# Up projections of block 1's gated FFNs with seven block products for eight, in a three-block decoder on one core

## The chip, the cores and the metric

One NeuronCore of a Trainium2 chip runs the whole program once. The metric is the device time of one execution in microseconds (us). The engines have their own queues: TensorE (PE, with its weight loads PEld), VectorE (DVE), ScalarE (ACT), GpSimd (POOL) and SyncE (SP), which here issues the loads of the weights. Each queue is worked off in its order. Results of TensorE land in banks of 128 partitions x 2 KB (PSUM); everything else works on SBUF.

## The reference, cut to what matters

Three blocks follow each other on 512 tokens of 1024 features, in the first block with 16 memory tokens ahead of them (528). Block 1 has two gated FFNs, one on 528 tokens and one on 512:

```
def swiglu(x, w_in, w_out):
    a, b = jnp.split(x @ w_in, 2, axis=-1)
    return (jax.nn.silu(a) * b) @ w_out

h = h + 0.5 * swiglu(rmsnorm(h, norm_ffn1), w_ffn1_in, w_ffn1_out)
...
h = h + 0.5 * swiglu(rmsnorm(h, norm_ffn2), w_ffn2_in, w_ffn2_out)
```

`w_in` is 1024 x 5632 and `w_out` 2816 x 1024: 22 pairs of gate and value blocks of 128 features each.

## The kernel before, in words

Features lie on partitions, tokens along the free axis. A residual stream of 8 tiles `h` [128, T] stays in SBUF. Each fp32 operand of a large product is split into a hi part in float32r (ScalarE, `activation Copy`) and a lo part, the rest (VectorE, `tensor_sub`), and a product is three matmuls: hi x hi, hi x lo, lo x hi (`mm3`, L248 to L252).

`wunit` (L232) loads a weight block of 128 output features, [128, 8 chunks, 128], on SP's queue (L239), and splits it: ScalarE L240, VectorE L244. Its three tiles have two buffers each. `block` (L258) runs one such unit over all chunks and, for 528 tokens, over two halves of 264 columns into two banks; for 512 tokens into one. There are eight banks.

`make_z` (L891) makes `zh`, `zl`, the split of `h` times the norm's gain. The norm's factor per token, `rs`, is made by `rstd` (L336) from sums of squares and is applied to the result of a projection, so the matmuls needn't wait for it.

`swiglu` (L369) goes over 22 pairs. For each, two blocks a (gate) and b (value); then for each half: VectorE multiplies a by `rs` (L380), ScalarE takes Silu (L381), GpSimd multiplies by `rs` (L382), VectorE multiplies by b (L384), and the result is split into `hh`, `hl` of that pair (L282, L287). After the loop, the down projection takes 8 output blocks over 22 chunks of `hh`, `hl`, and `done` (L928) adds half of it to `h`. The two blocks of pair 0 are issued ahead of `rs` (`ahead`, L254).

No order is written out by hand. The framework's scheduler takes the instructions in program order with their dependencies, and gives each engine a fixed order, in which one that is ready may go ahead of an earlier one that isn't; each engine then keeps that order on the chip. Buffers are handed on tile by tile.

Of the kernel before, what the change touches and what calls it, by code (L numbers as in the profile page):

```python
# [102 lines left out]
def arrays1(I, vec):  # L103
    """layouts for the first block"""
# [92 lines left out]
class Ctx:  # L197
# [13 lines left out]
    def psum(self, mm, s=0, t=0, o=0):  # L211
        """the banks: for projections, scores, transposes, and sums over several steps"""
# [19 lines left out]
    def wunit(self, src, kc, m=P):  # L232
        """src: DRAM AP [128, kc*m]; gives hi, lo tiles [128, kc, m]."""
# [60 lines left out]
    def stacked(self, out, x, s):  # L294
        """rows 64 s .. of x: hi parts in the same rows of out, lo parts in the other half"""
# [5 lines left out]
    def twice(self, hi, lo, x, s):  # L301
        """hi and lo parts of rows 64 s .. of x, each on both halves"""
# [7 lines left out]
    def unstack(self, out, ps):  # L310
        """the two halves of a bank added"""
# [13 lines left out]
    def sq_acc(self, acc, h, first, scale=1.0):  # L325
        """acc += (h * scale)^2"""
# [9 lines left out]
    def rstd(self, acc, halves, eps, name, pool=None, factor=None):  # L336
        """rstd of the columns, times factor if there is one, on all partitions: exp(-ln(mean + eps) / 2)"""
# [31 lines left out]
    def swiglu(self, w_up, w_dn, zs, rs, halves, hid, done):  # L369
        """w_up: DRAM [44, 128, 1024] with blocks a0 b0 a1 b1 ..; w_dn: [8, 128, 22*128]."""  # L370
        nc = self.nc
        T = rs.shape[1]
        for f in range(DFF):
            pa = self.block([(w_up[2 * f], KC)], zs, halves, key=2 * f)
            pb = self.block([(w_up[2 * f + 1], KC)], zs, halves, key=2 * f + 1)
            hh, hl = hid[f]
            for (s, z), a, b in zip(halves, pa, pb):
# [5 lines left out]
                tb = self.tp.tile([P, 512], F32, name="tb")[:, :z]  # L383
                nc.vector.tensor_mul(tb, b, ta)  # L384
                self.split(hh[:, c], hl[:, c], tb)
# [49 lines left out]
    def rstd_mm(self, sq, ones, eps, pool, name, psum=None):  # L435
        """exp(-ln(ones^T sq + eps) / 2), sq [128, <=512] fp32 (overwritten)"""
# [14 lines left out]
    def newton(self, r, ms, eps, u, spread=True):  # L451
        """one step for r ~ 1 / sqrt(ms + eps); u is scratch; spread: on three engines"""
# [11 lines left out]
    def head_sq(self, t, pool, bufs=2):  # L464
        """squares, and their hi and lo parts"""
# [8 lines left out]
    def head_fin(self, sq, halves, eps, pool, bufs=2, spread=False):  # L474
        """1 / sqrt of each head's mean"""
# [23 lines left out]
def act_tables(nc):  # L499
    """loads ScalarE's table sets where a function needs another one: the set that serves the most functions ahead"""  # L500
# [29 lines left out]
def mixer1(K, D, hs, zs, rs, work):  # L530
    """D: dict of DRAM APs and constant tiles. Gives mixed hi/lo (8 tiles, 512 tokens)."""
# [18 lines left out]
    def gate(n):  # L550
        """the projection of an output gate (0 .. of the attention, 8 .. of the retention, 16 .. of its output), kept in DRAM"""
# [17 lines left out]
    fst = ExitStack()  # L569
    ya = mb  # L570
    with tc.tile_pool(name="fox", bufs=1, reuse_waits="tile") as fp:
# [24 lines left out]
        def prep(j, res):  # L596
            """the operands of pair j, in stages"""
# [34 lines left out]
        def scores(j, s, ops):  # L632
            """softmax over each query tile's keys"""
# [49 lines left out]
        def forget(pf):  # L683
            """minus the cumulative sum of log_sigmoid, per head: the logarithms token-major, the memory last"""
# [206 lines left out]
def make_z(K, hs, gain, acc, T0=0, more=None, sq=True):  # L891
    """z = h * gain as hi/lo, and acc = sum of squares over the row blocks"""
# [19 lines left out]
def block1(K, D, tables):  # L912
# [9 lines left out]
    def ffn(zs, rs, halves, up, dn, T0):  # L922
        T = rs.shape[1]
        with tc.tile_pool(name="hid", bufs=1, reuse_waits="tile") as pool:
            hid = [(pool.tile([P, T], F32R, name=f"hh{f}"), pool.tile([P, T], F32R, name=f"hl{f}"))
                   for f in range(DFF)]

            def done(n, pl):  # L928
                for (s, z), p in zip(halves, pl):
# [1070 lines left out]
```

## Time and profile before

| what | value |
|---|---|
| median of 3 runs | 3465.2 us (3464.43 to 3467.01) |
| span of the profiled execution | 3469.6 us |
| the profiled execution's own time | the page gives the span alone |
| instructions | 45531 |
| matmuls | 17777 |
| HBM read | 288.22 MB |

The profile is of one execution. Its span runs from the first to the last instruction and stands 4.4 us above the median of the runs. Instructions are counted with their line in the kernel; a helper's line gathers many callers. "Idle before" names what ended the wait of an engine.

### The profile page before, as it was taken

What the parts mean: (1) busy time and instruction counts of PE and PEld (TensorE: products, weight loads), DVE (VectorE), ACT (ScalarE), POOL (GpSimd) and SP (SyncE); (2) the same over time, 40 slices, a digit from 0 to 9 for tenths busy, and PEclk for the clock granted to TensorE, in tenths of its full rate; (3) what the DMA queues carried; (4) which work ended last, traced back from release to release, by engine and by line L of the source; (5) the groups of instructions that cost most, each with busy time, mean ns of one, the idle gap of its engine ahead of it and who ended that gap; (6) DMA issues with size and microseconds to landing.
All of it is one profiled execution on the core that took longest, in us unless ns stands there. A gap on an engine that the chain in (4) does not pass through costs nothing. (4 is left out here: it accounts for less than half of the span.)

```text
span 3469.6 us, 45531 instructions
## 1 busy us (share of the span) xinstructions
PE 3344.1 (96%) x17777; PEld 2764.7 (80%) x17777; DVE 1955.4 (56%) x3248; ACT 1416.7 (41%) x2474; POOL 755.8 (22%) x786
## 2 busy tenths in 40 slices
PE   8999999999999999999999999999989998999999
PEld 7999977878777888867777778888878776768887
DVE  4443366656654443278776664666366656766642
ACT  3222366643333222245554333444334434654431
POOL 2211133321112111112211321111234432421100
PEclk9999999999999999999999999999999988999999
DMA  3323222232133333333332323333330012123233
GB/s 121 89 91 90 87 81 74 74 104 92 59 95 97 95 94 93 96 92 94 92 100 85 114 89 92 94 95 96 113 95 26 23 47 80 41 60 97 94 101 94
DMA packets 89590, 298.63 MB, mean 86 GB/s; under 512 B 10711, under 2 KB 11351, under 8 KB 89120
## 3 DMA queue, kind: packets, MB, share of 16 engines
q1 hardware_dynamic: 76896, 260.70, 24.5%
q0 software_dynamic: 6416, 23.80, 2.4%
q10 hardware_dynamic: 6064, 11.23, 1.0%
q8 instruction: 139, 2.28, 0.3%
q14 instruction: 75, 0.61, 0.1%
HBM read 288.22 MB, written 7.47 MB: 85 GB/s over the span
## 5 line engine op out<-in xcount | busy, mean ns | idle before, releaser
L250 PE MATMUL mm<-zh,wh 128*128 128x512 f32 (+1 forms) x3296 | 1187.4, 360 | 20.1 <-ACT zh L291 8.7
L252 PE MATMUL mm<-zh,wl 128*128 128x512 f32 (+1 forms) x3296 | 1190.1, 361 | 3.3 <-DVE wl L244 3.2
L251 PE MATMUL mm<-zl,wh 128*128 128x512 f32 (+1 forms) x3296 | 1182.7, 359 | 4.2 <-DVE zl L292 4.2
L240 ACT ACTIVATE wh<-w 128x1024 fp32r<-128x1024 f32 (+2 forms) x523 | 523.7, 1001 | 1088.7 <-PE mm L251 771.1
L244 DVE TENSOR_TENSOR wl<-w,wh 128x1024 fp32r<-128x1024 f32 (+2 forms) x523 | 626.1, 1198 | 400.0 <-ACT wh L240 391.1
L250 PEld LDWEIGHTS mm<-zh,wh 128*128 128x128 f32 x3296 | 621.8, 189 | 117.3 <-issue 9.1
L251 PEld LDWEIGHTS mm<-zl,wh 128*128 128x128 f32 x3296 | 623.1, 189 | 103.6 <-DVE zl L292 5.1
L252 PEld LDWEIGHTS mm<-zh,wl 128*128 128x128 f32 x3296 | 622.8, 189 | 95.8 <-DVE wl L244 6.4
L250 PE MATMUL mm<-hh,wh 128*128 128x512 f32 (+1 forms) x880 | 308.7, 351 | 0.0
L251 PE MATMUL mm<-hl,wh 128*128 128x512 f32 (+1 forms) x880 | 308.5, 351 | 0.0
L252 PE MATMUL mm<-hh,wl 128*128 128x512 f32 (+1 forms) x880 | 307.9, 350 | 0.0
L252 PEld LDWEIGHTS mm<-hh,wl 128*128 128x128 f32 x880 | 165.7, 188 | 23.3
L251 PEld LDWEIGHTS mm<-hl,wh 128*128 128x128 f32 x880 | 165.7, 188 | 23.1
L250 PEld LDWEIGHTS mm<-hh,wh 128*128 128x128 f32 x880 | 165.7, 188 | 23.1
L382 POOL TENSOR_TENSOR ta<-ta,rs 128x264 f32<-128x264 f32 (+1 forms) x66 | 85.9, 1314 | 395.7 <-ACT ta L381 395.7
L334 POOL TENSOR_TENSOR acc<-acc,ta 128x512 f32<-128x512 f32 (+1 forms) x49 | 83.4, 1703 | 350.3 <-ACT ta L333 349.9
L1000 POOL TENSOR_TENSOR cv<-cv 128x512 f32<-128x512 f32 x44 | 57.5, 1306 | 436.3 <-DVE cv L981 398.8
L981 DVE SCALAR_TENSOR_TENSOR cv<-ta,vec,cv 128x510 f32<-128x510 f32 (+1 forms) x176 | 132.0, 753 | 3.1 <-ACT cv L978 0.3
L384 DVE TENSOR_TENSOR tb<-mm,ta 128x264 f32<-128x264 f32 (+1 forms) x66 | 32.8, 519 | 142.1 <-PE mm L252 138.3
L995 DVE TENSOR_TENSOR ta<-mm,rs 128x512 f32<-128x512 f32 x88 | 60.3, 687 | 59.6 <-PE mm L252 59.5
L380 DVE TENSOR_TENSOR ta<-mm,rs 128x264 f32<-128x264 f32 (+1 forms) x66 | 32.5, 518 | 107.8 <-PE mm L252 107.8
L282 ACT ACTIVATE hh<-cv 128x512 fp32r<-128x512 f32 x44 | 27.8, 633 | 144.1 <-POOL cv L1000 144.1
(596 smaller groups left out, 4829.1 us busy)
## 6 DMA issues: line engine op xcount, KB each, us to landing
w<-in_w_up_dram SPq DMA_DIRECT2D x176, 512.0 KB, 3.5
w<-in_w_in_dram SPq DMA_DIRECT2D x160, 512.0 KB, 3.5
w<-in_w_dn_dram SPq DMA_DIRECT2D x64, 512.0 KB, 3.5
w<-in_w_dn_dram SPq DMA_DIRECT2D x32, 384.0 KB, 3.1
w<-in_w_out_dram SPq DMA_DIRECT2D x16, 512.0 KB, 3.6
aB<-acum_d POOLq DMA_DIRECT2D x16, 512.0 KB, 6.0
w<-in_w_pb_dram SPq DMA_DIRECT2D x32, 256.0 KB, 3.0
negc<-negc_d POOLq DMA_DIRECT2D x8, 528.0 KB, 4.1
```

What stands on the lines that cost most here:

```text
L240: nc.scalar.activation(h_, w_, AF.Copy)
L244: nc.vector.tensor_sub(l_, w_, h_.bitcast(F32))
L250: nc.tensor.matmul(ps, wh, xh, start=start, stop=False)
L251: nc.tensor.matmul(ps, wh, xl, start=False, stop=False)
L252: nc.tensor.matmul(ps, wl, xh, start=False, stop=stop)
L334: nc.gpsimd.tensor_tensor(acc, acc, q, op=ALU.add)
L380: nc.vector.tensor_mul(ta, a, rs[:, c])
L382: nc.gpsimd.tensor_tensor(ta, ta, rs[:, c], op=ALU.mult)
L384: nc.vector.tensor_mul(tb, b, ta)
L981: nc.vector.scalar_tensor_tensor(y[:, d:], x[:, :T - d], w(i), y[:, d:], op0=ALU.mult, op1=ALU.add)
L995: nc.vector.tensor_mul(x, p, rs)
L1000: nc.gpsimd.tensor_tensor(y[1], y[1], y[0], op=ALU.mult)
```

## The change

The value of 19 of the 22 pairs is computed as a 2x2 block product in seven products (Winograd's form of Strassen's method). The 2x2 blocks: rows are the gate block a and the value block b, the inner dimension is cut in chunks 0 to 3 and 4 to 7, columns are the left and the right half of the tokens (264 or 256 columns). Each product is 4 chunks x 3 matmuls.

- The first three pairs (`ords=3`) stay as they are, except that the result is stored as fp32 and not split.
- `combos(k)`: for chunk k and k + 4, `h` times gain times `rs` (so the norm's factor is now inside), as four quarters in `F`, then four subtractions on GpSimd, then the split of seven pieces. It is called for k = 0 to 3 in the course of the first two ordinary pairs.
- `weights(f)`: loads a and b of the pair (two DMAs, a tile `b32` more with two buffers), makes their combinations `s12` (GpSimd) and `s34` (half VectorE, half GpSimd), and splits a whole unit of a, `s12`, `s34` and half a unit of b.
- `fast(f)`: seven products P1 to P7 into three banks a, b, c, with partial results added in between by VectorE (`w`, `y`, the right value `x_R`, the right gate, the left value) and ScalarE (a copy, two Silu), and gate times value on GpSimd at the end. In the prediction `x_R` is the addition after P5, which reads bank b before P7 adds to it; u0 to u3 are the weights of P1 and P4, P2 and P3, P5 and P6, P7.
- The results of all 22 pairs stay in fp32, in the tiles that held `zh`, `zl` and in six more. After the loop they are split, all 22, into tiles that lie where the scratch of the fast pairs was; then the down projection goes as before.
- Docstrings and comments are taken out elsewhere in the file, which shifts no instruction.

```
-    def swiglu(self, w_up, w_dn, zs, rs, halves, hid, done):
-        for f in range(DFF):
+    def swiglu(self, w_up, w_dn, zs, rs, hs, gain, done, ords=3):
+        hp = pool(left, "hx")
+        seven = ExitStack()
+        bp = pool(seven, "b32")
+        cz = pool(seven, "cz")
...
+        def ordinary(f):
             pa = self.block([(w_up[2 * f], KC)], zs, halves, key=2 * f)
             pb = self.block([(w_up[2 * f + 1], KC)], zs, halves, key=2 * f + 1)
-            hh, hl = hid[f]
+            x = tile_of(f)
             for (s, z), a, b in zip(halves, pa, pb):
                 c = slice(s, s + z)
                 ta = self.tp.tile([P, 512], F32, name="ta")[:, :z]
                 nc.vector.tensor_mul(ta, a, rs[:, c])
                 nc.scalar.activation(ta, ta, AF.Silu)
                 nc.gpsimd.tensor_tensor(ta, ta, rs[:, c], op=ALU.mult)
-                tb = self.tp.tile([P, 512], F32, name="tb")[:, :z]
-                nc.vector.tensor_mul(tb, b, ta)
-                self.split(hh[:, c], hl[:, c], tb)
+                nc.vector.tensor_mul(x[:, c], b, ta)
+            return x
+
+        def combos(k, fp):
+            F = fp.tile([P, 8, h], F32, name="F", bufs=2)
+            v = lambda x: x.rearrange("p (a b) -> p a b", a=2)
+            for n, o in ((k, F[:, 0:8:7]), (k + 4, F[:, 1:3])):
+                nc.vector.scalar_tensor_tensor(o, v(hs[n]), gain(n), v(rs), op0=ALU.mult, op1=ALU.mult)
+            for o, x, y in ((3, 7, 0), (4, 2, 3), (5, 2, 7), (6, 1, 4)):
+                nc.gpsimd.tensor_tensor(F[:, o], F[:, x], F[:, y], op=ALU.subtract)
+            zh = cz.tile([P, 7, h], F32R, name=f"ch{k}")
+            zl = cz.tile([P, 7, h], F32R, name=f"cl{k}")
+            self.split(zh, zl, F[:, :7])
+            ck.append((zh, zl))
+
+        def weights(f, sp):
+            wa = self.wp.tile([P, KC, P], F32, name="w32", bufs=2)
+            wb = bp.tile([P, KC, P], F32, name="b32", bufs=2)
+            nc.sync.dma_start(wa.rearrange("p a b -> p (a b)"), w_up[2 * f])
+            nc.sync.dma_start(wb.rearrange("p a b -> p (a b)"), w_up[2 * f + 1])
+            u0 = [self.wp.tile([P, KC, P], F32R, name=n) for n in ("wh", "wl")]
+            split_unit(u0, wa)
+            s12 = sp.tile([P, KC, P], F32, name="s12")
+            s34 = sp.tile([P, KC, P], F32, name="s34")
+            sub = lambda o, x, y, op=ALU.subtract: nc.gpsimd.tensor_tensor(o, x, y, op=op)
+            sub(s12[:, :4], wb[:, :4], wb[:, 4:], ALU.add)
+            sub(s12[:, 4:], s12[:, :4], wa[:, :4])
+            u1 = [sp.tile([P, KC, P], F32R, name=n, bufs=2) for n in ("uh", "ul")]
+            split_unit(u1, s12)
+            nc.vector.tensor_sub(s34[:, :4], wa[:, :4], wb[:, :4])
+            sub(s34[:, 4:], wa[:, 4:], s12[:, 4:])
+            u2 = [sp.tile([P, KC, P], F32R, name=n, bufs=2) for n in ("uh", "ul")]
+            split_unit(u2, s34)
+            u3 = [self.wp.tile([P, KC, P], F32R, name=n)[:, :4] for n in ("wh", "wl")]
+            split_unit(u3, wb[:, 4:])
+            return u0, u1, u2, u3
+
+        def product(ps, u, at, b, first):
+            for k in range(4):
+                wh, wl = u[0][:, at + k], u[1][:, at + k]
+                xh, xl = ck[k][0][:, b], ck[k][1][:, b]
+                kw = dict(skip_group_check=True)
+                nc.tensor.matmul(ps, wh, xh, start=first and k == 0, stop=False, **kw)
+                nc.tensor.matmul(ps, wh, xl, start=False, stop=False, **kw)
+                nc.tensor.matmul(ps, wl, xh, start=False, stop=k == 3, **kw)
+
+        def fast(f, sp):
+            u0, u1, u2, u3 = weights(f, sp)
+            a, b, c = (self.pp.tile([P, 512], F32, name="mm")[:, :h] for _ in range(3))
...
+            product(a, u0, 0, 0, True)
+            nc.scalar.activation(m, a, AF.Copy)
+            product(b, u1, 4, 4, True)
+            nc.vector.tensor_add(w, b, m)
+            product(c, u1, 0, 3, True)
+            nc.vector.tensor_add(y, c, m)
+            product(a, u0, 4, 1, False)
+            nc.scalar.activation(g[:, lr[0]], a, AF.Silu)
+            product(b, u2, 0, 5, False)
+            nc.vector.tensor_add(x[:, lr[1]], b, y)
+            product(c, u2, 4, 2, False)
+            nc.vector.tensor_add(g[:, lr[1]], c, w)
+            nc.scalar.activation(g[:, lr[1]], g[:, lr[1]], AF.Silu)
+            product(b, u3, 0, 6, False)
+            nc.vector.tensor_add(x[:, lr[0]], b, m)
+            nc.gpsimd.tensor_tensor(x, x, g, op=ALU.mult)
+            return x
+
+        with tc.tile_pool(name="F", bufs=1, reuse_waits="tile", side="right") as fp:
+            for f in range(ords):
+                xs.append(ordinary(f))
+                if f < 2:
+                    combos(2 * f, fp)
+                    combos(2 * f + 1, fp)
+        sp = pool(right, "sw", "right")
+        for f in range(ords, DFF):
+            xs.append(fast(f, sp))
+        right.close()
+        seven.close()
+        h0, h1 = pool(right, "hr", "right"), pool(left, "hl")
+        hid = []
+        for f in range(DFF):
+            hid.append([(h0 if f < 8 else h1).tile([P, T], F32R, name=f"h{e}{f}") for e in "hl"])
+            self.split(*hid[f], xs[f])
         for n in range(KC):
             d = w_dn[n]
             pn = self.block([(d[:, :1024], 8), (d[:, 1024:2048], 8), (d[:, 2048:], 6)], hid, halves)
             done(n, pn)
...
-    ffn(zs, rs, H2, D["w_up1"], D["w_dn1"], 0)
+    ffn(zs, rs, H2, D["w_up1"], D["w_dn1"], 0, lambda n: V("norm_ffn1", n))
...
-    ffn(zs, rs, [(0, 512)], D["w_up2"], D["w_dn2"], 16)
+    ffn(zs, rs, [(0, 512)], D["w_up2"], D["w_dn2"], 16, lambda n: V("norm_ffn2", n))
```

## Rows read from the trace of the kernel before

**Rows 1.** The page, busy us of each engine, share of the span and count.

```profile
PE 3344.1 (96%) x17777; PEld 2764.7 (80%) x17777; DVE 1955.4 (56%) x3248; ACT 1416.7 (41%) x2474; POOL 755.8 (22%) x786
```

**Rows 2.** Stretches of the two up phases: length, busy us of PE PEld DVE ACT POOL, clock.

```profile
58.10:279.00 220.90, 220.90 (x1826) 220.90 (x1825) 89.74 (x152) 64.11 (x114) 41.71 (x38) 1.00 0.30 91
1133.00:1344.00 211.00, 211.00 (x915) 171.44 (x914) 84.86 (x97) 61.57 (x78) 34.03 (x19) 1.00 0.31 95
```

**Rows 3.** Timeline of VectorE, L380 19 pairs apart (start us, us, engine, line).

```profile
52.29 0.79 DVE L380 TENSOR_TENSOR ta<-mm,rs 128x264 f32<-128x264 f32 x2 [2.57 <-PE mm L252]
...
273.20 0.79 DVE L380 TENSOR_TENSOR ta<-mm,rs 128x264 f32<-128x264 f32 x2 [2.52 <-PE mm L252]
...
1137.72 0.69 DVE L380 TENSOR_TENSOR ta<-mm,rs 128x512 f32<-128x512 f32 x1 [2.44 <-PE mm L252]
...
1348.49 0.69 DVE L380 TENSOR_TENSOR ta<-mm,rs 128x512 f32<-128x512 f32 x1 [2.81 <-PE mm L252]
```

**Rows 4.** Waits of PE from 1070 to 1470 us, all there are.

```profile
PE mm L250 <- DVE h L956: 0.9, 1, 0.9
```

**Rows 5.** Timeline of PE, three matmuls of 256 columns in a row.

```profile
856.60 0.37 PE L250 MATMUL s<-rqh,rkh 128*128 128x256 f32 x1
856.80 0.28 PE L251 MATMUL s<-rql,rkh 128*128 128x256 f32 x1
856.92 0.28 PE L252 MATMUL s<-rqh,rkl 128*128 128x256 f32 x1
```

**Rows 6.** Lengths: groups by form (mean ns), and by tile or line (shortest/median/longest ns).

```profile
L240 ACT ACTIVATE wh<-w 128x1024 fp32r<-128x1024 f32 x440 | 465.2, 1057 | 916.2 <-PE mm L251 667.8 <-issue 229.6 <-DMA w<-in_w_in_dram 11.3
L282 ACT ACTIVATE hh<-tb 128x512 fp32r<-128x512 f32 x22 | 13.9, 632 | 2.1 <-DVE tb L384 2.1
L287 DVE TENSOR_TENSOR hl<-tb,hh 128x512 fp32r<-128x512 f32 x22 | 15.0, 684 | 0.7 <-ACT hh L282 0.7
...
L244 DVE TENSOR_TENSOR wl<-w,wh x523: 293/1225/2370, 10.2 to 3456.6; 128x1024 fp32r<-128x1024 f32 x147, 128x512 fp32r<-128x512 f32 x19, 128x768 fp32r<-128x768 f32 x8, 128x256 fp32r<-128x256 f32 x1
L384 DVE TENSOR_TENSOR tb<-mm,ta x66: 431/433/692, 36.6 to 1354.1; 128x264 f32<-128x264 f32 x44, 128x512 f32<-128x512 f32 x22
L382 POOL TENSOR_TENSOR ta<-ta,rs x66: 741/1486/1797, 35.9 to 1350.0; 128x264 f32<-128x264 f32 x44, 128x512 f32<-128x512 f32 x22
```

**Rows 7.** Timelines of VectorE and GpSimd, operations that meet and ones that don't.

```profile
1349.39 1.23 DVE L244 TENSOR_TENSOR wl<-w,wh 128x1024 fp32r<-128x1024 f32 x1 [0.21 <-ACT wh L240]
1349.98 1.80 POOL L382 TENSOR_TENSOR ta<-ta,rs 128x512 f32<-128x512 f32 x1 [9.30 <-ACT ta L381]
...
1076.89 1.87 DVE L292 SCALAR_TENSOR_TENSOR zl<-h,vec,zh 128x512 fp32r<-128x512 f32 x1
1076.92 1.29 POOL L334 TENSOR_TENSOR acc<-acc,ta 128x512 f32<-128x512 f32 x1 [11.43 <-ACT ta L333]
...
1082.49 0.75 DVE L292 SCALAR_TENSOR_TENSOR zl<-h,vec,zh 128x512 fp32r<-128x512 f32 x1
```

**Rows 8.** Timeline of VectorE: rs finished (L462), third pair's last bank read (L384).

```profile
34.15 0.77 DVE L462 SCALAR_TENSOR_TENSOR rs<-ta,rs 128x264 f32<-128x264 f32 x2
...
58.16 0.79 DVE L384 TENSOR_TENSOR tb<-mm,ta 128x264 f32<-128x264 f32 x2 [3.26 <-PE mm L252]
...
1125.58 0.69 DVE L462 SCALAR_TENSOR_TENSOR rs<-ta,rs 128x512 f32<-128x512 f32 x1
...
1143.33 0.69 DVE L384 TENSOR_TENSOR tb<-mm,ta 128x512 f32<-128x512 f32 x1 [3.49 <-PE mm L252]
```

**Rows 9.** Timeline of PE after a wait, and that stretch's row (columns of rows 2).

```profile
33.26 0.22 PE L1349 MATMUL mm<-oh,rb 33*8 33x16 f32 x2 [1.67 <-DVE ta L460]
33.57 0.59 PE L250 MATMUL mm<-zh,wh 128*128 128x264 f32 x1
...
36.37 0.36 PE L250 MATMUL mm<-zh,wh 128*128 128x264 f32 x1
...
30.00:40.00 10.00, 8.24 (x48) 6.70 (x47) 5.69 (x13) 4.33 (x12) 1.99 (x3) 0.83 0.20 56
```

More of the change, by code (lines that the diff above doesn't have):

```diff
@@ L366, in eps, with pool, tile_of @@
         return self._eps[v]
-    def swiglu(self, w_up, w_dn, zs, rs, halves, hid, done):
-        nc = self.nc
+    def swiglu(self, w_up, w_dn, zs, rs, hs, gain, done, ords=3):
+        nc, tc = self.nc, self.tc
         T = rs.shape[1]
-        for f in range(DFF):
+        h = T // 2
+        lr = [slice(0, h), slice(h, T)]
+        left, right = ExitStack(), ExitStack()
+        def pool(st, name, side="left"):
+            return st.enter_context(tc.tile_pool(name=name, bufs=1, reuse_waits="tile", side=side))
+        hp = pool(left, "hx")
+        seven = ExitStack()
+        bp = pool(seven, "b32")
+        cz = pool(seven, "cz")
+        def tile_of(f):
+            i = f - ords
+            if 0 <= i < 16:
+                return self.zp.tile([P, 528], F32, name=f"z{'hl'[i % 2]}{i // 2}")[:, :T]
+            return hp.tile([P, T], F32, name=f"hx{f}")
+        def ordinary(f):
+            halves = [(0, h), (h, h)] if T > 512 else [(0, T)]
             pa = self.block([(w_up[2 * f], KC)], zs, halves, key=2 * f)
             pb = self.block([(w_up[2 * f + 1], KC)], zs, halves, key=2 * f + 1)
-            hh, hl = hid[f]
+            x = tile_of(f)
             for (s, z), a, b in zip(halves, pa, pb):
@@ L382, in swiglu @@
                 nc.gpsimd.tensor_tensor(ta, ta, rs[:, c], op=ALU.mult)
[L383 to L385 removed]
+                nc.vector.tensor_mul(x[:, c], b, ta)
+            return x
+        ck = []
+        def combos(k, fp):
[9 more added lines that the diff above has]
+            ck.append((zh, zl))
@@ new lines, in split_unit @@
+        def split_unit(hl, x):
+            r = "p a b -> p (a b)"
+            self.split(hl[0].rearrange(r), hl[1].rearrange(r), x.rearrange(r))
+        def weights(f, sp):
[19 more added lines that the diff above has]
+            return u0, u1, u2, u3
@@ new lines, in product @@
+        def product(ps, u, at, b, first):
[9 more added lines that the diff above has]
+            a, b, c = (self.pp.tile([P, 512], F32, name="mm")[:, :h] for _ in range(3))
+            x = tile_of(f)
+            g = self.tp.tile([P, 528], F32, name="ta")[:, :T]
+            m = sp.tile([P, 264], F32, name="m1", bufs=2)[:, :h]
+            wx = self.tp.tile([P, 528], F32, name="tb")[:, :T]
+            w, y = wx[:, :h], wx[:, h:]
+            product(a, u0, 0, 0, True)
[15 more added lines that the diff above has]
+            return x
@@ new lines, in swiglu @@
+        xs = []
+        with tc.tile_pool(name="F", bufs=1, reuse_waits="tile", side="right") as fp:
[10 more added lines that the diff above has]
+        h0, h1 = pool(right, "hr", "right"), pool(left, "hl")
@@ L386, in swiglu @@
+        hid = []
+        for f in range(DFF):
+            hid.append([(h0 if f < 8 else h1).tile([P, T], F32R, name=f"h{e}{f}") for e in "hl"])
+            self.split(*hid[f], xs[f])
+        halves = [(0, h), (h, h)] if T > 512 else [(0, T)]
         for n in range(KC):
@@ L389, in swiglu @@
             done(n, pn)
+        right.close()
+        left.close()
     def setup_consts(self, c):
@@ L920, in block1, with ffn, done @@
         nc.sync.dma_start(hs[n], D["x"][n])
-    def ffn(zs, rs, halves, up, dn, T0):
+    def ffn(zs, rs, halves, up, dn, T0, gain):
         T = rs.shape[1]
[L924 to L929, printed above, removed]
-                    c = hs[n][:, T0 + s:T0 + s + z]
-                    nc.vector.scalar_tensor_tensor(c, p, 0.5, c, op0=ALU.mult, op1=ALU.add)
-            K.swiglu(up, dn, zs, rs, halves, hid, done)
+        def done(n, pl):
+            for (s, z), p in zip(halves, pl):
+                c = hs[n][:, T0 + s:T0 + s + z]
+                nc.vector.scalar_tensor_tensor(c, p, 0.5, c, op0=ALU.mult, op1=ALU.add)
+        K.swiglu(up, dn, zs, rs, [h[:, T0:T0 + T] for h in hs], gain, done)
     acc = new_acc(K, 528)
```

## The prediction

> **What bounds the kernel now.** Read first the busy times, then the stretches of the two up phases, then their repetition, then who waits. TensorE is busy 96% of the span, VectorE 56%, GpSimd 22% [rows 1]. In both up phases TensorE is busy in the whole of its stretch at granted clock 1.00, that is at 2.4 GHz, while VectorE stands at 40% and GpSimd below 20% [rows 2]. So the time of these phases is a count of matmuls times their distance. The same step of a pair recurs 19 pairs apart at 52.29 and 273.20 us in the first FFN, at 1137.72 and 1348.49 us in the second [rows 3]: 220.91 / 19 = 11.627 us and 210.77 / 19 = 11.093 us a pair. Over 96 matmuls of 264 columns that is 0.1211 us each, over 48 of 512 columns 0.2311 us. From 1070 to 1470 us TensorE has one wait, of 0.9 us, ahead of the second up phase [rows 4]; the wait before the first ends at 33.26 us [rows 9]. No wait is there to be won; only columns are.
>
> **Columns.** A fast pair issues 7 products x 4 chunks x 3 = 84 matmuls of half the tokens; 19 of 22 pairs are fast. First FFN: 84 x 0.1211 = 10.17 us, a gain of 1.45 us a pair, 27.6 us in 19. Second FFN: 256 columns lie near 264, and the line through 0.1211 and 0.2311 us gives 0.1176 us; three such matmuls in a row started 0.12 us apart [rows 5]. At 0.119 a pair costs 10.0 us and gains 1.09, 20.7 us in all; the ends are 0.1176 (23.0 us) and 0.1211 (17.5 us). I take 20: **-47.6 us** together.
>
> **New work beside it, per fast pair.** Lengths are undisturbed ones [rows 6]. ScalarE: three hi parts at 1.06, one of half width at 0.63, a copy and two Silu of half the tokens, under 0.63 each: 5.7 us. VectorE: three lo parts at 1.225, one at 0.69, half of s34 at 0.69, five additions out of banks at 0.43: 7.2 us. GpSimd: three combinations of 512 columns and one product x*g at 1.29 [rows 7]: 5.2 us. Each alone is under 10 us. But two of them meet. A VectorE lo part from 1349.39 to 1350.62 makes a GpSimd product begun at 1349.98 last 1.80 us, where another of its size took 1.29; and a VectorE scaling begun just ahead of a GpSimd addition took 1.87 us, where the same beside none takes 0.75 [rows 7]. So the later of the two waits for the earlier when both read SBUF twice. The bank additions, with one SBUF operand, show none of this: 0.43 at the shortest and in the median. What must share is then 3 x 1.225 + 2 x 0.69 = 5.06 us of VectorE and 5.16 of GpSimd: 10.2 us of recorded length against 10.17 of TensorE. The overlap of the pair at 1349.39 (2.39 us where the lengths add to 2.52) takes 5% off: 9.7 us. It fits, narrowly. The Trainium skill's page "SBUF — State Buffer", section "Who interferes with whom", states the same as a rule: a two-SBUF-input VectorE instruction and a GpSimd one that reads SBUF exclude each other wholly. By that rule the sum would be 10.2 us and TensorE would just lose its lead; the 1.80 us agrees with it but for the 5%.
>
> Laying one pair out by these lengths (products of 1.45 us, P1 at 0, P4 ending at 5.8): u0's buffer is free at 5.8; Silu, then its hi part end at 7.5; its lo part, behind one addition and one GpSimd operation, ends near 9.0, needed at 10.15. The addition x_R follows P5 at 7.25 and frees bank b by 7.7, needed by P7 at 8.7. u1 has 4.8 us to spare, u2 likewise. So no wait when the order suits; I book 0.1 us a pair, **+4 us**. The ends are 0 and 0.75 (below, the second rival).
>
> The DMAs are the same blocks (two of 512 KB a pair) on SP's queue, now every 10.2 us for 11.6, with two buffers more; the queue gets ahead of need, at no cost. If it didn't, each pair would wait for a block.
>
> **The start of the fast pairs.** Product 1 needs all four combos and these need rs. First FFN: rs is done at 34.92 us, the third ordinary pair leaves TensorE at 58.16: a window of 23.2 us. Second: 1126.27 to 1143.33, 17.1 us [rows 8]. Work that shares the port until then: GpSimd 16 subtractions of half the tokens at 0.74 [rows 6] and three ordinary products, 15 us; VectorE eight scalings at 0.75 [rows 7], four lo parts of 1848 columns (by the line through 512 and 1024 columns 2.09 each), three weight parts at 1.225: 18 us. Undivided 33 us, with 5% off 31. The need is 1.1 us after the window. The first FFN would be late by 6.6 us, the second by 13. Lower ends by VectorE alone (18 and 5 of bank work, 23 us): 0 to 1 and 5 to 6. Part of GpSimd's 15 us falls beside the 5 us of bank work, so I take 5 and 10. After a wait of 1.67 us TensorE ran 13 matmuls 0.22 us apart in place of 0.12 (33.57 to 36.37 us, granted clock 0.83 in that stretch: 1.2 GHz for a part of it) [rows 9]; 13 x 0.1 = 1.3 us, here taken as 1.5 each. **+18 us**, ends 8 and 26.
>
> **The hand-over to the down projection.** Before, each pair's split ran inside the loop. Now 22 splits stand after it, 22 x 0.68 = 15 us of VectorE and 22 x 0.63 = 14 of ScalarE [rows 6], ahead in the code of the first down weights. Some ten can run in the last pair, as its scratch comes free; then the down phase eats a split per 0.7 us. Weights for its second unit, needed 5.8 us in, wait for u3's buffers and stand behind twelve splits (12 x 0.68 + 1.225 = 9.4 us): 3.6 us late, with the slower clock 5. Lower end 0, if those weights go first. I take 4 each, **+8 us**, ends 0 and 13. What leaves the pairs, 44 halves of splits, was hidden and gives nothing.
>
> **Sum.** -47.6 + 4 + 18 + 8 = -17.6 us on a profiled span of 3469.6, 3452.0. That span is 4.4 us above the median of the runs, 3465.2; so **3447.6 us**. Its own ends, with 512-to-256 columns, start and hand-over: about 3437 to 3458.
>
> **Rivals.** (1) *All hidden*: order and overlap cover start and hand-over to some 5 us; 3465.2 - 47.6 + 5 = 3423. For it: VectorE is at 40%. Against it: the 17.1 us window. Chance 0.17. (2) *x_R behind a lo part*: VectorE's queue keeps its order, and if u0's lo part stands before x_R, it ends at 8.95, x_R at 9.4, and P7 waits 0.7 us in each of 38 pairs; 28 for the 4 booked: 3472. Chance 0.20. (3) *Slower: the port becomes the bound.* If the bank additions (2.1 us a pair) also stand still whenever VectorE's queue waits for GpSimd, a pair takes up to 7.2 + 5.2 = 12.4 us; halfway to 10.2 it is 11.3, that is 0.3 less than before in the first FFN and 0.2 more in the second: the gain is gone, start and hand-over remain, 3465.2 + 26 - 2 = 3489, and at 12.4 some 3530. It decides from (11.36 - 26/38) = 10.7 us a pair. The rule of the skill's page pulls to this side. Chance 0.20. (4) *No fewer columns' worth of time*: 84 matmuls for 48 in the second FFN would break even at 11.093 / 84 = 0.132 us each; the 0.12 of [rows 5] speaks against it. With the first FFN alone gaining: 3465.2 - 27.6 + 30 = 3468. Chance 0.03. The forecast keeps 0.40.
>
> **Numbers.** The measurement tells about 0.2%, 7 us, from no change. Faster by more (under 3458): nearly all of the forecast, all of rival 1, a little of 2: 0.58. Same: 0.15, mostly of rival 2. Slower (over 3472): 0.27, rival 3 and half of 2. Range 3424 to 3495: it leaves out half of rival 1 and the upper half of rival 3.
>
> **What would show it.** Right: up phases busy throughout, a pair recurring every 10.2 and 10.0 us, one gap of 5 to 10 us ahead of each first fast pair ended by VectorE's lo part of the last combo, and a gap of some 4 us early in each down phase. Rival 2: a short wait in every pair for the addition x_R. Rival 3: pairs over 10.7 us, VectorE operations at twice their length beside GpSimd, TensorE waiting for lo parts. Wrong altogether if the time moves outside block 1's FFNs.

## The result, and the profile after

The median is 3506.7 us (3476.0 to 3514.7, 8 runs) beside 3466.1 us for the kernel before in the same session (3455.2 to 3470.9, 8 runs): a ratio of 1.0116, interval 1.0088 to 1.0143. The change costs 40.6 us, where 17.6 us of gain were forecast; 3506.7 lies above the range's 3495. The profiled execution of the changed kernel spans 3498.9 us and took 3500.6 us.

To see where the time went, both FFNs were cut at the same five events, all on VectorE: the end of rs, and the starts of the last bank read of the third ordinary pair, of the last addition of the last pair, and of the first and the last output of the down projection.

| stretch (us) | FFN 1 before | after | FFN 2 before | after | change in both |
|---|---|---|---|---|---|
| rs to third pair | 23.24 | 41.79 | 17.06 | 32.73 | +34.2 |
| 19 pairs | 220.91 | 213.32 | 210.78 | 208.92 | -9.5 |
| hand-over to first output | 15.94 | 23.25 | 15.26 | 22.93 | +15.0 |
| rest of the down projection | 111.90 | 111.57 | 107.36 | 106.34 | -1.4 |

The sum, +38.4 us, lies near the +40.6 us of the runs; the two profiled spans differ by 29.3 us only. The rest is that parts which the change doesn't touch took less in the execution after: the stretch between the two FFNs 715.5 us for 719.4, the part behind the second 1989.3 for 1992.9. Over the profiled executions of this study that last part took from 1971 to 1994 us. In experiments 2 and 6 the profiled execution lies 20 and 18 us under the median of its runs, and this part stands at the low end. So kernels are compared below by their timed ratios and by these stretches, not by their spans, and the pairs' times are those of one execution.

The changed kernel's page, busy us, share, count; it answers to [rows 1]:

```profile
PE 3318.1 (95%) x18233; PEld 2767.0 (79%) x18233; DVE 2210.8 (63%) x3440; ACT 1508.6 (43%) x2593; POOL 966.8 (28%) x913
```

TensorE's busy time fell by 26 us and the time still rose. The stretches, in the columns of [rows 2], show where it isn't busy:

```profile
33.00:76.00 43.00, 30.23 (x196) 29.26 (x196) 32.05 (x33) 14.60 (x16) 36.37 (x28) 0.78 0.12 38
76.00:288.00 212.00, 197.57 (x1590) 193.99 (x1589) 180.88 (x185) 90.34 (x130) 113.00 (x70) 1.00 0.29 88
288.00:312.00 24.00, 20.29 (x141) 19.66 (x141) 18.45 (x28) 14.73 (x26) 1.30 (x1) 0.86 0.24 72
1139.00:1172.00 33.00, 22.29 (x77) 16.84 (x76) 25.05 (x21) 11.89 (x11) 25.44 (x20) 0.84 0.10 32
1172.00:1380.00 208.00, 197.53 (x1593) 193.91 (x1593) 181.11 (x190) 91.06 (x132) 118.84 (x75) 0.98 0.31 93
1380.00:1403.00 23.00, 19.43 (x71) 14.92 (x71) 17.66 (x26) 14.29 (x25) 1.27 (x1) 0.85 0.24 74
```

**The pairs.** Against [rows 2], TensorE is now idle for 14.4 us in 212, and VectorE went from 41% to 85%. The recurrence, the left value's addition L479 of each pair, answers to [rows 3]; the rows of two pairs in the first FFN and four in the second:

```profile
86.63 0.43 DVE L479 TENSOR_TENSOR zh<-mm,m 128x264 f32<-128x264 f32 x1
97.95 0.43 DVE L479 TENSOR_TENSOR zl<-mm,m 128x264 f32<-128x264 f32 x1
...
1188.33 0.41 DVE L479 TENSOR_TENSOR zh<-mm,m 128x256 f32<-128x256 f32 x1
1199.48 0.41 DVE L479 TENSOR_TENSOR zl<-mm,m 128x256 f32<-128x256 f32 x1
...
1300.27 0.41 DVE L479 TENSOR_TENSOR zh<-mm,m 128x256 f32<-128x256 f32 x1
1310.48 0.41 DVE L479 TENSOR_TENSOR zl<-mm,m 128x256 f32<-128x256 f32 x1
```

In the first FFN it is 11.32 to 11.34 us a pair, in the second 11.16 to 11.19 us up to 1289 us and 10.2 us from 1300 us on: one program, two rhythms in one execution. (In each FFN the last two pairs are shorter.) TensorE's waits from 90 to 260 us, in the form of [rows 4]:

```profile
PE mm L453 <- DVE zl L474: 6.8, 8, 0.9
PE mm L453 <- DVE zh L474: 6.0, 7, 0.9
```

So one wait of 0.85 us in each of these 15 pairs, and always for x_R (L474). The timeline of one pair, all engines:

```profile
104.74 1.29 POOL L435 TENSOR_TENSOR s<-b 128x512 f32<-128x512 f32 x1 [3.56 <-DVE ul L287]
...
104.82 2.30 DVE L287 TENSOR_TENSOR wl<-w,wh 128x1024 fp32r<-128x1024 f32 x1 [0.21 <-ACT wh L282]
...
106.11 2.14 POOL L435 TENSOR_TENSOR s<-s,w 128x512 f32<-128x512 f32 x1
...
106.38 0.28 PE L455 MATMUL mm<-ch,ul 128*128 128x264 f32 x1
...
107.04 0.42 DVE L474 TENSOR_TENSOR zh<-mm,tb 128x264 f32<-128x264 f32 x1
...
107.51 0.40 PE L453 MATMUL mm<-ch,wh 128*128 128x264 f32 x1 [0.85 <-DVE zh L474]
...
107.74 0.29 PE L454 MATMUL mm<-cl,wh 128*128 128x264 f32 x1
```

GpSimd's first combination begins 0.08 us ahead of VectorE's lo part of u0. The lo part, 1.225 us long when undisturbed [rows 6], takes 2.30. Behind it in VectorE's queue stands x_R, whose bank has long been ready; behind x_R waits P7, which adds into that bank. From P6's last matmul at 106.38 to P7's second at 107.74 it is 1.36 us where 0.24 would do: 1.12 us, the whole distance between 11.32 and 10.2. In the other rhythm the two lo parts are back to back, GpSimd's combination comes second and takes the delay, and x_R is in time:

```profile
1314.81 1.21 DVE L287 TENSOR_TENSOR ul<-s,uh 128x1024 fp32r<-128x1024 f32 x1
1315.94 1.21 DVE L287 TENSOR_TENSOR wl<-w,wh 128x1024 fp32r<-128x1024 f32 x1
1317.08 0.41 DVE L474 TENSOR_TENSOR zh<-mm,tb 128x256 f32<-128x256 f32 x1
...
1316.15 2.15 POOL L435 TENSOR_TENSOR s<-b 128x512 f32<-128x512 f32 x1 [2.48 <-DVE ul L287]
```

**The start.** TensorE's long waits, timeline; [rows 9] had one, of 1.67 us:

```profile
48.34 0.39 PE L250 MATMUL mm<-zh,wh 128*128 128x264 f32 x1 [3.13 <-ACT wh L240]
...
55.25 0.81 PE L252 MATMUL mm<-zh,wl 128*128 128x264 f32 x2 [4.71 <-DVE wl L244]
...
67.40 0.81 PE L252 MATMUL mm<-zh,wl 128*128 128x264 f32 x2 [4.93 <-DVE wl L244]
...
1148.79 0.79 PE L252 MATMUL mm<-zh,wl 128*128 128x512 f32 x1 [3.75 <-DVE wl L244]
...
1171.59 0.58 PE L455 MATMUL mm<-ch,wl 128*128 128x256 f32 x1 [4.37 <-DVE wl L287]
```

The gap was expected ahead of the first fast pair; four of these five lie among the ordinary pairs, and wait for the weights of an ordinary pair. The timelines of VectorE and GpSimd tell why:

```profile
47.06 2.08 DVE L287 TENSOR_TENSOR cl<-F,ch 128x1848 fp32r<-128x1848 f32 x1 [2.42 <-ACT ch L282]
49.06 1.93 DVE L414 SCALAR_TENSOR_TENSOR F<-h,vec,rs 128x528 f32<-128x528 f32 x2
...
53.44 1.76 DVE L244 TENSOR_TENSOR wl<-w,wh 128x1024 fp32r<-128x1024 f32 x1
...
50.39 10.20 POOL L416 TENSOR_TENSOR F<-F 128x264 f32<-128x264 f32 x8 [0.65 <-DVE F L414]
```

The lo part that ends TensorE's wait at 55.25 stands behind a combination's lo part, ahead of which VectorE had sat idle for 2.42 us for the hi part on ScalarE, and behind scalings and a bank read. Beside it eight subtractions took 10.20 us, 1.28 each in the mean where 0.74 was booked. In the mean of these stretches the granted clock is 0.78 over 43 us and 0.84 over 33, that is 1.2 GHz for part of them.

**The hand-over.** Timelines of ScalarE and TensorE:

```profile
283.91 1.06 ACT L240 ACTIVATE wh<-w 128x1024 fp32r<-128x1024 f32 x1 [3.92 <-PE mm L454]
...
288.31 1.06 ACT L240 ACTIVATE wh<-w 128x1024 fp32r<-128x1024 f32 x1 [0.47 <-PE mm L454]
289.28 1.69 ACT L282 ACTIVATE hh<-hx 128x528 fp32r<-128x528 f32 x3
...
289.96 0.51 PE L250 MATMUL mm<-hh,wh 128*128 128x264 f32 x2 [1.61 <-ACT hh L282]
...
292.02 0.59 PE L251 MATMUL mm<-hl,wh 128*128 128x264 f32 x1 [1.55 <-DVE hl L287]
```

The down weights went ahead of the splits, and no split ran before the last pair was done. TensorE waits 1.61 and 1.55 us for the first ones and once 0.55 us for a later unit; the granted clock is 0.86 over 24 us, which is another 24 x 0.14 = 3.4 us if TensorE is taken as busy all the while. Together some 7.1 of the 7.3 us.

### The profile page after: what moved, and what is told of

Same layout as the page of the kernel before. It is cut to its first block, busy times and chain, and to the rows that moved or that the text cites. A ratio compares the mean times of both kernels' runs of the same rounds, so it can differ in the third digit from the quotient of the medians.

```text
span 3498.9 us, 47078 instructions
## 1 busy us (share of the span) xinstructions
PE 3318.1 (95%) x18233; PEld 2767.0 (79%) x18233; DVE 2210.8 (63%) x3440; ACT 1508.6 (43%) x2593; POOL 966.8 (28%) x913
## 3 DMA queue, kind: packets, MB, share of 16 engines
q1 hardware_dynamic: 76896, 260.70, 23.8%
## 5 line engine op out<-in xcount | busy, mean ns | idle before, releaser
L252 PE MATMUL mm<-zh,wl 128*128 128x512 f32 (+2 forms) x2384 | 899.9, 378 | 20.8 <-DVE wl L244 20.7
L250 PE MATMUL mm<-zh,wh 128*128 128x512 f32 (+2 forms) x2384 | 897.8, 377 | 22.9 <-ACT zh L291 8.4
L251 PE MATMUL mm<-zl,wh 128*128 128x512 f32 (+2 forms) x2384 | 891.8, 374 | 3.5 <-DVE zl L292 3.5
L250 PEld LDWEIGHTS mm<-zh,wh 128*128 128x128 f32 (+1 forms) x2384 | 453.0, 190 | 108.5 <-issue 9.1
L252 PEld LDWEIGHTS mm<-zh,wl 128*128 128x128 f32 (+1 forms) x2384 | 452.5, 190 | 102.6 <-DVE wl L244 25.1
L251 PEld LDWEIGHTS mm<-zl,wh 128*128 128x128 f32 (+1 forms) x2384 | 453.5, 190 | 88.2 <-DVE zl L292 4.2
L453 PE MATMUL mm<-ch,uh 128*128 128x264 f32 (+1 forms) x608 | 173.7, 286 | 1.4 <-ACT uh L282 1.4
L455 PE MATMUL mm<-ch,ul 128*128 128x264 f32 (+1 forms) x608 | 173.0, 285 | 0.1
L454 PE MATMUL mm<-cl,uh 128*128 128x264 f32 (+1 forms) x608 | 172.7, 284 | 0.0
L453 PE MATMUL mm<-ch,wh 128*128 128x264 f32 (+1 forms) x456 | 133.5, 293 | 23.8 <-DVE zl L474 11.5
```

The source lines that it names most:

```text
L250: nc.tensor.matmul(ps, wh, xh, start=start, stop=False)
L251: nc.tensor.matmul(ps, wh, xl, start=False, stop=False)
L252: nc.tensor.matmul(ps, wl, xh, start=False, stop=stop)
L453: nc.tensor.matmul(ps, wh, xh, start=first and k == 0, stop=False, **kw)
L454: nc.tensor.matmul(ps, wh, xl, start=False, stop=False, **kw)
L455: nc.tensor.matmul(ps, wl, xh, start=False, stop=k == 3, **kw)
```

## The experiments

**Theory**: (a) in each pair the meeting of GpSimd's combination and VectorE's lo part holds x_R, and P7 behind it; (b) the start is a backlog ahead of the ordinary weights; (c) the hand-over is splits that come late. **Rival** on (a): the port (what VectorE and GpSimd must share in the prediction's sum), or VectorE, has no more capacity than one pair in 11.3 us. "Excess of start" is the stretch from rs to the last ordinary pair, less what the kernel before takes for as many pairs.

**1. P5 ahead of P4**, which puts two products between x_R's read of bank b and P7:

```
-            product(a, u0, 4, 1, False)
-            nc.scalar.activation(g[:, lr[0]], a, AF.Silu)
             product(b, u2, 0, 5, False)
             nc.vector.tensor_add(x[:, lr[1]], b, y)
+            product(a, u0, 4, 1, False)
+            nc.scalar.activation(g[:, lr[0]], a, AF.Silu)
```

> Product P5 is issued ahead of P4, so that bank b has two products (2.9 us) in place of one (1.45 us) between P5 and P7 for the addition x_R. Theory of the order (x_R stands behind a lo part that waits for GpSimd's port): the wait of 0.85 us a pair goes, pairs recur every 10.2 us in both FFNs in place of 11.3 and 11.2 to 10.2, some 30 us less than the changed kernel, near 3475 us. Rival, port at its limit (the work of VectorE and GpSimd that shares it needs 11.3 us a pair): pairs stay at 11.3 us and the wait turns up at another instruction, near 3505 us. Between them: u0's buffers come free one product later, so a wait for u0's lo part of up to 0.7 us a pair could take its place, near 3495 us.

Measured: 3497.9 us (6 runs), ratio 1.0087 (1.0059 to 1.0116); 11.1 us a pair in the first FFN. TensorE's waits from 90 to 260 us:

```profile
PE mm L453 <- DVE tb L468: 11.1, 16, 1.1
```

The wait for x_R is gone, and one of 0.7 us in the mean stands ahead of P5, which now has only P3 between itself and w's read of bank b (L468). At 112.38 us, for one, w stands behind two operations of VectorE that take 1.72 and 1.81 us beside GpSimd, where 0.69 is their undisturbed length. The order of products moves the wait to whichever bank is turned round within one product; it doesn't remove it. Taken alone this is nearer to the rival than to the theory: the pairs stayed over 11 us and the wait turned up elsewhere, and the ratio's interval overlaps that of the changed kernel. Experiments 5 and 8 decide between the two.

**2. The combinations spread over five ordinary pairs**, one set behind each of the first four:

```
-    ... done, ords=3):
+    ... done, ords=5):
-                if f < 2:
-                    combos(2 * f, fp)
-                    combos(2 * f + 1, fp)
+                if f < 4:
+                    combos(f, fp)
```

> Five ordinary pairs in place of three, and one combo behind each of the first four in place of two behind each of the first two. Theory of the backlog (31 us of work that shares the port against windows of 23 and 17 us): two pairs add 23 and 22 us of window, the waits for weights among the ordinary pairs and for the combos, 17 and 16 us, fall to under 3 us each; two pairs less in each FFN give back about 3 us; near 3480 us. Rival, chain (each combo's scaling, subtractions, hi and lo part hold up the weights behind them in VectorE's queue, whatever the window): waits fall by a third only, near 3497 us.

Measured: 3475.6 us (12 runs), ratio 1.0013 (0.9996 to 1.003). Excess of start 9.9 and 13.6 us for 18.6 and 15.7; TensorE's long waits at the first start fell to 1.68, 2.10 and 0.74 us, at the second waits of 8.6 us in all are left. The pairs ran at 11.32 us in the first FFN and at 10.21 throughout the second, so much of the gain is the other rhythm. (b) is borne out in part: the excess fell to half in the first FFN and by 2.1 us in the second, by a third in the two together, which is what the rival had said of the waits. The window matters, but so does the chain through which a combination goes.

**3. Ordinary pairs split at once**, into the down projection's own tiles, as before the change:

```
-            x = tile_of(f)
+            x = [hp.tile([P, T], F32R, name=f"hy{e}{f}") for e in "hl"]
...
-                nc.vector.tensor_mul(x[:, c], b, ta)
+                tb = self.tp.tile([P, 512], F32, name="tb")[:, :z]
+                nc.vector.tensor_mul(tb, b, ta)
+                self.split(x[0][:, c], x[1][:, c], tb)
...
+            if f < ords:
+                hid.append(xs[f])
+                continue
```

> The three ordinary pairs of each FFN are split at once, as before the change, so that only 19 splits stand behind the loop and TensorE has three pairs (2.2 us of work) ahead of the first of them. Theory (the 7 us of each hand-over are the first late split's latency, two waits of 1.6 us, and the slower clock after them): the two waits go and the clock stays, some 12 us less than the changed kernel, near 3495 us. Rival, rate (the splits feed TensorE too slowly whatever its head start, or the down weights are late): under 4 us less, near 3505 us.

Measured: 3494.9 us (6 runs), ratio 1.0073 (1.0045 to 1.01). Hand-over 19.5 and 19.3 us for 23.3 and 22.9, with waits of 1.3, 0.7 and 0.5 us left in the first; that is 7.4 us of the gain. In the profiled execution another 12.8 us are pairs of 10.2 us in the second FFN, a rhythm that this edit doesn't bear on, and the start took 4.3 us more. Three split pairs give TensorE something to begin with. (c) stands.

**4. All three edits, then the last two.**

> P5 ahead of P4, five ordinary pairs with one combo behind each of four, and the ordinary pairs split at once, together. If the three causes stand beside each other the gains add: 3507 - 30 - 27 - 12, near 3438 us, under the 3466 of the kernel before. Where the port is at its limit, 3507 - 27 - 12, near 3468 us.

Measured: 3486.2 us (12 runs), ratio 1.0051 (1.0035 to 1.0066). A miss of both figures: with P5 first the pairs take 10.9 to 11.2 us in both FFNs.

> Five ordinary pairs with one combo behind each of four, and the ordinary pairs split at once; the products in the order of the changed kernel. The two causes lie at different places, so their gains add: 32 and 12 us off 3507, near 3463 us, at or just under the kernel before. Pairs as in the five-pair run: 11.3 us in the first FFN, 10.2 in the second. If the head start of five split pairs brings nothing beyond the waits it removes, near 3470 us.

Measured: 3473.9 us (12 runs), ratio 1.0027 (1.0012 to 1.0041). That is above both figures. The first FFN ran at 11.36 us and from 214 us on at 10.3; the second stayed at 11.17. In experiment 2, the same pair code, it was the second that ran fast: which rhythm a FFN is in is not set by its size.

**5. A fourth bank**, on top of the last: P7 gets a bank of its own, for one addition more on VectorE.

```
-            a, b, c = (self.pp.tile([P, 512], F32, name="mm")[:, :h] for _ in range(3))
+            a, b, c, d = (self.pp.tile([P, 512], F32, name="mm")[:, :h] for _ in range(4))
...
+            nc.vector.tensor_add(y, b, m)
...
-            product(b, u3, 0, 6, False)
-            nc.vector.tensor_add(x[:, lr[0]], b, m)
+            product(d, u3, 0, 6, True)
+            nc.vector.tensor_add(x[:, lr[0]], d, y)
```

> As the run before it, and P7 goes into a bank of its own, added to b + m by one VectorE addition more (0.43 us), so that no product of a pair waits for x_R. Theory of the turnaround (TensorE loses 0.85 us and a tenth of a us of restart where one product lies between two uses of a bank and VectorE is in a lo part that waits for the port): pairs of the first FFN fall from 11.3 to 10.2 to 10.4 us, 17 x 1.0 = 17 us, near 3446 us; the second FFN stays at 10.2. Rival, port at its limit in the first FFN: pairs stay at 11.3 us or above, since VectorE has more to do, and TensorE waits for a lo part instead, near 3463 us or above.

Measured: 3468.5 us (12 runs), ratio 0.9997 (0.998 to 1.0013). The pairs take 10.3 and 10.2 us but for two of 10.5, and between 90 and 260 us the list of TensorE's waits is empty. The left value's addition, a pair apart in each FFN:

```profile
122.21 0.42 DVE L482 TENSOR_TENSOR zh<-mm,tb 128x264 f32<-128x264 f32 x1
132.52 0.42 DVE L482 TENSOR_TENSOR zl<-mm,tb 128x264 f32<-128x264 f32 x1
...
1204.59 0.41 DVE L482 TENSOR_TENSOR zh<-mm,tb 128x256 f32<-128x256 f32 x1
1214.80 0.41 DVE L482 TENSOR_TENSOR zl<-mm,tb 128x256 f32<-128x256 f32 x1
```

All of GpSimd's work and 0.4 us more of VectorE's are still there: capacity is not what made 11.3, and the rival falls. The 3446 us weren't reached, because the hand-over rose from 18.2 to 25.1 and 23.8 us. Its waits on TensorE's timeline:

```profile
274.17 0.59 PE L250 MATMUL mm<-hh,wh 128*128 128x264 f32 x1 [3.27 <-ACT wh L240]
...
277.78 0.81 PE L252 MATMUL mm<-hh,wl 128*128 128x264 f32 x2 [2.36 <-DVE wl L244]
```

Here the splits do run ahead of the second unit of down weights, and it is the weights that are late.

**6. The weight combinations on VectorE**, on top of experiment 4's second kernel:

```
-            sub = lambda o, x, y, op=ALU.subtract: nc.gpsimd.tensor_tensor(
+            sub = lambda o, x, y, op=ALU.subtract: nc.vector.tensor_tensor(
```

> As the first run of this call, with the three weight combinations of a pair on VectorE in place of GpSimd. VectorE's own work goes from 7.2 to 9.3 us a pair, GpSimd keeps one product of 1.3 us, so almost nothing meets at the port. Theory of the port with the order (the 2.3 us lo part ahead of x_R is 1.2 us without a GpSimd operation in its way): the wait for x_R falls under 0.3 us and pairs of the first FFN take 10.2 to 10.6 us, near 3450 us. Rival, VectorE's queue alone (it is the late engine whoever does the combinations): pairs of 11 us or more in both FFNs, near 3475 us.

Measured: 3458.5 us (12 runs), ratio 0.9974 (0.9957 to 0.9992): below the kernel before. The pairs take 10.5 and 10.3 us.

**7. A second buffer for s12**, on top of experiment 2:

```
-            s12 = sp.tile([P, KC, P], F32, name="s12")
+            s12 = sp.tile([P, KC, P], F32, name="s12", bufs=2)
```

> Five ordinary pairs with one combo behind each of four, without the split at once, and two buffers for s12, so that GpSimd's combination for the next pair no longer starts in the moment in which VectorE's lo part of the one before ends, just ahead of the lo part of u0. Theory of the moment (GpSimd takes the port 0.08 us ahead of that lo part in the pairs of 11.3 us): the lo part takes 1.2 us in place of 2.3, pairs of the first FFN fall to 10.2 us, some 17 us under the five-pair run, near 3459 us. Rival: the two meet elsewhere and pairs stay at 11.3 us, near 3476 us.

Measured: 3482.5 us (8 runs), ratio 1.0041 (1.0025 to 1.0056); 11.06 and 10.89 us a pair. TensorE's timeline in a pair:

```profile
110.69 0.39 PE L453 MATMUL mm<-ch,wh 128*128 128x264 f32 x1 [0.58 <-DVE zl L474]
```

A miss: GpSimd is freed from one wait and meets VectorE elsewhere; x_R is still late, by less.

**8. The same edit as 6 on the changed kernel alone**, which leaves the code of start and hand-over as the change made it:

> The changed kernel with the three weight combinations of each pair on VectorE instead of GpSimd, and nothing else. Theory: the pairs' 1.1 us is the meeting of the two engines followed by VectorE's queue, so it goes here: pairs of 10.3 to 10.6 us, no TensorE wait for x_R, 2 x 19 x 0.8 = 30 us less than the changed kernel, near 3476 us; start (42 and 33 us) and hand-over (23 us) stay as they were. Rival: VectorE's own 1.9 us more a pair put x_R later still, pairs of 11.3 us or more, 3505 us or slower.

Measured: 3475.6 us (12 runs), ratio 1.0028 (1.0012 to 1.0044). From 1.0116 that is 0.88%, 30 us. The pairs take 10.52 and 10.27 us, the hand-over 22.2 and 21.7, the excess of start 15.5 and 15.7 for 18.6 and 15.7; 23 of the 30 us lie in the pairs. A stretch and three operations of VectorE:

```profile
100.00:200.00 100.00, 99.34 (x800) 97.28 (x799) 91.76 (x124) 47.18 (x68) 14.82 (x9) 1.00 0.32 98
```

```profile
153.88 0.69 DVE L435 TENSOR_TENSOR s<-b 128x512 f32<-128x512 f32 x1
154.49 1.22 DVE L287 TENSOR_TENSOR wl<-w,wh 128x1024 fp32r<-128x1024 f32 x1
155.62 0.42 DVE L474 TENSOR_TENSOR zl<-mm,tb 128x264 f32<-128x264 f32 x1
```

VectorE is busier than in the same stretch of the changed kernel, 91.8 us of 100 for 88.8, and the pair is 0.8 us shorter: the lo part that stands ahead of x_R takes 1.22 us, and a combination takes VectorE 0.69 us where GpSimd took 1.29. x_R still stands behind it, which costs TensorE 0.3 us at P7.

**9. Four ordinary pairs**, otherwise experiment 6:

> The weight combinations on VectorE, the ordinary pairs split at once, four ordinary pairs with one set of combinations behind each, 18 fast pairs. Theory: against the 3458.5 us of the kernel with five ordinary pairs, one more fast pair saves 0.8 us of columns in each FFN (11.1 to 10.3), the start costs more of TensorE's waits, since the combinations' lo parts stand closer together: same within 6 us. Rival: the start's waits depend on the total backlog alone, 3457 us.

Measured: 3461.6 us (12 runs), ratio 0.9996 (0.9981 to 1.0012). Both FFNs together take 2.6 us more than with five, with an excess of start of 13.2 and 13.4 us for 10.4 and 13.5. The timed ratios are 0.0022 apart, 7.6 us, a little outside what was expected; their intervals overlap.

**10. Experiments 5 and 6 together.**

> The weight combinations on VectorE together with the fourth bank. Theory: both take the same wait out of the pairs, so they don't add: pairs of 10.2 to 10.4 us, no wait inside a pair; the hand-over shows whether the late splits running ahead of the down weights go with the fourth bank (25 us, as it had) or with the engine (18 us): 3458 to 3472 us. Rival: VectorE, which gets 1.9 us and 0.5 us more a pair, is late: pairs of 10.8 us or more, 3470 us or slower.

Measured: 3459.1 us (12 runs), ratio 0.9975 (0.9958 to 0.9992). The addition into the left value, a pair apart in each FFN:

```profile
110.45 0.42 DVE L482 TENSOR_TENSOR zl<-mm,tb 128x264 f32<-128x264 f32 x1
120.63 0.42 DVE L482 TENSOR_TENSOR zh<-mm,tb 128x264 f32<-128x264 f32 x1
...
1255.56 0.42 DVE L482 TENSOR_TENSOR zh<-mm,tb 128x256 f32<-128x256 f32 x1
1265.53 0.41 DVE L482 TENSOR_TENSOR zl<-mm,tb 128x256 f32<-128x256 f32 x1
```

```profile
100.00:200.00 100.00, 100.00 (x827) 100.00 (x827) 95.55 (x138) 46.54 (x69) 16.62 (x10) 1.00 0.34 103
```

10.18 and 9.97 us, with TensorE busy in the whole of the stretch beside a VectorE at 96%: this is TensorE's own price of a pair. The hand-over takes 24.1 and 23.7 us, so its growth goes with the fourth bank. A fourth bank with the down weights issued ahead of the splits wasn't tried.

**11. The subtractions of the normed values on VectorE too**, on top of experiment 6:

```
-                nc.gpsimd.tensor_tensor(F[:, o], F[:, x], F[:, y], op=ALU.subtract)
+                nc.vector.tensor_tensor(F[:, o], F[:, x], F[:, y], op=ALU.subtract)
```

> As the kernel with the weight combinations on VectorE (3458.5 us), and the four subtractions of each set of combinations of the normed values on VectorE too, so that GpSimd has none of the change's subtractions. Theory: during the ordinary pairs both engines slow each other down (a subtraction of 1.5 us took up to 10 us on GpSimd, a lo part 2.4 us); with VectorE alone the 5 to 8 us of start that are left shrink: 3450 us. Rival: VectorE's queue itself is the backlog (16 subtractions of about 0.4 us are added to it), the start becomes longer by 2 to 5 us in each FFN: 3463 us.

Measured: 3448.4 us (8 runs) beside 3464.0 us, ratio 0.995 (0.9932 to 0.9968), the fastest here. The excess of start is 5.4 and 9.8 us for 10.4 and 13.5. What is left of TensorE's long waits at the first start:

```profile
48.79 0.39 PE L250 MATMUL mm<-zh,wh 128*128 128x264 f32 x1 [0.55 <-ACT wh L240]
...
51.04 0.51 PE L252 MATMUL mm<-zh,wl 128*128 128x264 f32 x2 [1.50 <-DVE wl L244]
```

VectorE does more work and the start is shorter, so the amount of work isn't what cost there. Whether it was the meetings or the longer way over GpSimd (a subtraction takes VectorE 0.42 us where none meets it, GpSimd 0.74) isn't separated. The 10 us of the expectation are eight subtractions together, the x8 of the row above; the longest single one took 2.6 us.

## Why the prediction was wrong, point by point

| term | forecast (us) | measured (us) | from |
|---|---|---|---|
| columns | -47.6 | -48.8 | 19 x (11.627 - 10.18) + 19 x (11.093 - 9.97), experiment 10 |
| in the pair | +4 | +32.9 | 19 x (11.21 - 10.18) + 19 x (10.67 - 9.97), means of the last 18 pairs after |
| start | +18 | +40.8 | 34.2, and 6.6 by which the two first fast pairs are longer than that mean |
| hand-over | +8 | +15.0 | the stretches |

With -1.4 in the rest of the down projection the sum is +38.5, as found.

**Columns**: right, for both widths. 84 matmuls cost 0.1212 us each at 264 columns and 0.1187 at 256, where 0.1211 and 0.119 were taken.

**In the pair**: this is the step that failed, "So no wait when the order suits; I book 0.1 us a pair". Its capacity argument, 9.7 us of shared port in 10.17 us of TensorE, held: experiment 5 runs that work in 10.30 and 10.22 us with no wait listed. But a pair isn't limited by capacity alone. Bank b has one product, 1.45 us, in which to be read, and VectorE keeps its order. The layout put x_R ahead of u0's lo part, and took the lo part at its undisturbed length; on the chip the lo part stood ahead, as in the second rival, at 2.30 us, by the meeting the third rival speaks of. The second rival's price, 0.7 us in each pair for the position alone, was too high: without a meeting the position costs 0.3 (experiment 8). With it, 1.12 us. Neither rival had the two together; the third one's 11.3 us met the measured 11.32 by luck, since its reason, a bound port, is refuted by experiment 5.

What the port did leave is small: 10.22 us a pair in experiment 5's second FFN against 9.97 where GpSimd has no combinations. The Trainium skill's page "SBUF — State Buffer", section "Who interferes with whom", makes the two engines exclude each other. The ends of the operations agree with it: the lo part held at 104.82 ends 1.09 us behind GpSimd's end at 106.03. So the page's rule gave the size of a meeting; what a meeting costs depended on who stood behind it. The sum of 10.2 us a pair is not what bounds experiment 5: in ten pairs of its second FFN, 102.2 us, the recorded operations of both engines that work on SBUF alone cover 94.1 us.

**Start**: a cause was named rightly, the combinations' work; its size and its place were not. 40.8 us lie above the upper end of 26, which is itself 3 us more than its own figures give (6.6 + 13 + 2 x 1.5). The prediction let all waiting fall ahead of the first fast pair, as one sum of port work. In fact the combinations delayed the ordinary pairs' own weights, several times, with the clock at 0.78 and 0.84 in the stretch, and in the first FFN VectorE idled 1.75 to 2.43 us ahead of each combination's lo part for a hi part of ScalarE, which a sum of busy times doesn't hold. Experiments 2 and 11 take back 11 and a further 9 us in both FFNs together; the 15 us that are left are not explained by a run.

**Hand-over**: twice the size, and the other way round. Forecast were weights behind splits; found were splits behind weights and behind the last pair. The forecast mechanism exists: experiment 5 turned it on, and it is no cheaper.

**Sign**: 0.27 had been given to slower. The upper ends of the terms together, -47.6 + 28.5 + 26 + 13, give +20 us, some 3485, under the range's end of 3495; each of the three lies above its own end. They have in common that lengths were summed and the order in the queues was taken as the convenient one, in the pair, among the ordinary pairs' weights and at the hand-over.

## What to carry to other kernels

When a change moves work beside a saturated engine, sum the lengths to see whether it fits, then look for the buffer with the shortest turnaround and ask what can stand ahead of its reader in that reader's queue, at the disturbed length. Where two engines exclude each other and the tight read is on one of them, it can pay to let that one do both shares: here moving three GpSimd operations to a VectorE already at 89% made a pair 0.8 us shorter. And a reordering that handed the tight wait to another bank brought a pair from 11.3 to 11.1 us; a spare bank removed it.

## What the runs showed of the hardware that was not expected

- Who is first decides: GpSimd 0.08 us ahead, and the lo part takes 2.30 us for 1.21; the other way round, GpSimd's combination takes 2.15 us for 1.29 and TensorE loses 0.24 us of a pair (10.21 us for 9.97). In the traces after, of experiments 2, 3, 5 and 7 and of the second kernel of 4, a whole lo part and a combination of 512 columns meet with starts at most 0.35 us apart 138 times. In the 137 with starts over 0.01 us apart, the earlier kept its length (1.23 us at most, 1.32 for GpSimd) and the later took 2.03 us or more. The prediction's second example in [rows 7], a scaling held to 1.87 us though it began 0.03 us ahead, is another operation and doesn't follow this.
- The order reproduces itself from pair to pair: 11.32 to 11.34 us over 17 pairs without an exception, then in another FFN a change from 11.17 to 10.2 us within one execution, of the same instructions. What sets it off was not found. It may be a source of the spread of the changed kernel's runs (3476 to 3515 us); that was not shown, and the part behind the second FFN alone varied by 23 us.
- Under constant meetings GpSimd's subtraction of 264 columns took 1.28 us in the mean of eight, for 0.74 undisturbed.
- The slower clock at the hand-over (0.86 over 24 us, 3.4 us in the first FFN) cost about as much as the 3.7 us of waits in the same stretch.
